# A decoder block on one core: three weight units instead of two in the program's first loads, from two queues

## The chip, the core and the metric

The kernel runs on one core of a Trainium2 chip. The core has five engines that run side by side: TensorE (PE in the profile; its weight loads are listed as PEld), VectorE (DVE), ScalarE (ACT), GpSimd (POOL) and SyncE (SP), which issues the transfers between HBM and the on-chip memory. Each engine works off its own list of instructions in order, and semaphores hold an instruction back until its operands are there. The metric is the device time of one execution in microseconds: 543.99 us, the median of three runs (543.96 to 544.42).

## The reference

One layer on 256 tokens of width 1024, in float32: a gated feed-forward block (width 2816), a mixing layer of two branches (attention over the tokens so far, and a spatial gating in chunks of 128), a second feed-forward block, and a last norm. The change touches the beginning, the first feed-forward block:

```python
def rmsnorm(x, g):
    y = xf * lax.rsqrt(jnp.mean(xf * xf, axis=-1, keepdims=True) + EPS)
    return (y * g.astype(jnp.float32)).astype(x.dtype)
def swiglu(x, w_gate, w_up, w_down):
    return (jax.nn.silu(x @ w_gate) * (x @ w_up)) @ w_down
h = h + 0.5 * swiglu(rmsnorm(h, ffn1_norm[l]), ffn1_w_gate[l], ffn1_w_up[l], ffn1_w_down[l])
```

## The kernel before

Every float32 operand of a product is split in two: a high part (the value cast to float32r) and a low part (the value minus its high part). A product is then high x high, high x low and low x high. The moving operand of the first feed-forward block is the input, turned (feature on the partitions, 256 tokens along the row), with its high and its low part side by side. So one product of 512 columns (`mm_high`, L159) gives high x high and high x low in two halves of a bank of PSUM, and one of 256 columns (`mm_low`, L164) adds low x high. `collect` (L189) brings a bank back: ScalarE copies the second half into a small buffer `lo` (of which there are two), and VectorE adds it to the first half.

Weights come in units. A unit of the first block (f1) holds 256 columns over all of K = 1024: 128 gate columns and the 128 up columns that belong to them, in 8 blocks of K. It takes 2 banks ("sides") and 2 x 8 products of either kind. Two rings hold weights: `rawp`, seven buffers of half a unit as loaded (512 KB each, SP issues them in order as buffers come free), and `wp`, four buffers of a whole unit, split (w0, w1, ... in the rows below; w4 takes the buffer of w0). `split` (L198) casts the high part on ScalarE (L199) and subtracts on VectorE (L200). `unit(i, ahead)` has units i to i + ahead split.

The first two units don't come that way. The array `first` in HBM holds the gain of the norm and, for each of the 8 blocks of K, the block's rows of the turned input (256 columns) and of the first two units (256 columns each). Seven pieces and a last one are loaded by SP in order (`load_front`, `CUTS`). For each block, ScalarE multiplies the input by the gain (L354, the high part), VectorE makes its low part (L355), and the two units are split. TensorE takes the blocks as they come: for each block, the four sides' high products and then the four sides' low products (`by_passes` with one block of K).

The input is multiplied by the gain alone at that point; the root mean square is applied behind the products. For it, the input comes once more in rows (tile h, L362), ScalarE squares it in four halves (`square_sum`, L233; tile sq), VectorE makes a mean for each 128 tokens (L240, L241; ms), GpSimd its power of -0.5 (L243; rstd), and TensorE turns the two columns rstd into a row over tokens (`rows_of`, L250; tile rows). These two turns stand in TensorE's list right behind the products of unit 3 and ahead of those of unit 4 (f1g4, f1u4). The results of units 0 to 3 wait in the tile `first` until the scale is there; from unit 4 on it is applied at once.

TensorE's and SP's lists are in the order in which the code is written. The lists of ScalarE, VectorE and GpSimd are put in order by a scheduler when the program is built, so an edit can move instructions that it doesn't name. Ahead of all, 14 products of zeros (`WARM`, L93) keep TensorE at work until the first data is there.

```python
for group in ((0, 1), (2,), (3,)):
    ...
    for ks in ([k] for k in range(KB)) if len(group) > 1 else (range(KB),):
        by_passes(sides, ks)
    for f, i in at:
        collect(first[:, f, i, :], ps[f, i])
rs = []
for j in range(NT):
    for hf in range(2):
        square_sum(h, j, hf, "1")
    rs.append(rstd_of(j, "1"))
rows = rows_of(rs, "1")
```

Of the kernel before, what the change touches and what calls it, by code (L numbers as in the profile page):

```python
# [32 lines left out]
FIRST = 2  # L33
# [6 lines left out]
CUTS = (0, 1, 2, 3, 4, 6, 7, 8)  # L40
# [3 lines left out]
def block_kernel(ctx, tc, t, out):  # L44
# [22 lines left out]

    ROW = S + FIRST * UC
    front = act.tile([P, FB * S], F32, tag="aTh", name="front")
    back = act.tile([P, ROW], F32, tag="nC", name="back")  # L70

    def load_front(k, end, c0=0, c1=ROW):

        a, b = KB * (k + c0 > 0) + k * ROW + c0, KB + (end - 1) * ROW + c1
        to = back[:, c0:c1] if k == KB - 1 else front[:, a:b]
        nc.sync.dma_start(to, t["first"][:, a:b])

    load_front(0, 1, 0, S + UC)
    load_front(0, 1, S + UC, ROW)
# [86 lines left out]
    def by_passes(sides, ks=range(KB)):  # L166
# [11 lines left out]
        if KB - 1 in ks:  # L178
            for ps, of in sides:
                (sh, _), both = of(KB - 1)  # L180
                mm_high(ps, sh, both, False, True)

# [26 lines left out]
    def block_of(nT, k):  # L209
        return both_of(nT, k)[:, 0, :], both_of(nT, k)[:, 1, :]  # L210
# [129 lines left out]
    def in_front(k, end):  # L340
        if k == KB - 1:
            return back.rearrange("p (k c) -> p k c", k=1)
        return front[:, KB + k * ROW:KB + end * ROW].rearrange("p (k c) -> p k c", k=end - k)

    for i in range(FIRST):
        unit_tile(i)
    for k, end in zip(CUTS, CUTS[1:]):
        if k:
            load_front(k, end)
        rows_of_k = in_front(k, end)  # L350
        for q in range(end - k):
            g = front[:, k + q:k + q + 1]
            hi, lo = block_of(nT, k + q)
            nc.scalar.activation(hi, rows_of_k[:, q, :S], AF.Identity, scale=g)  # L354
            nc.vector.scalar_tensor_tensor(lo, rows_of_k[:, q, :S], g, hi.bitcast(F32),  # L355
                                           op0=ALU.mult, op1=ALU.subtract)
        for i in range(2):
            w = parts[i]
            split(w[:, k:end, 0, :], w[:, k:end, 1, :], rows_of_k[:, :, S + i * UC:S + (i + 1) * UC])
# [5 lines left out]
    for group in ((0, 1), (2,), (3,)):  # L365
        at = [(f, i) for f in group for i in range(2)]
        w = {f: unit(f1 + f, PAIRED if len(group) > 1 else ALONE) for f in group}
# [3 lines left out]
        for ks in ([k] for k in range(KB)) if len(group) > 1 else (range(KB),):  # L371
            by_passes(sides, ks)
# [340 lines left out]
```

## Time and profile before

| | |
|---|---|
| median of 3 runs | 543.99 us (543.96 to 544.42) |
| the profiled execution | 544.41 us |
| its span, first to last instruction | 542.7 us |
| mean granted TensorE clock | 0.996 |
| PE, DVE, ACT busy | 533.7, 388.9, 304.3 us |
| moved by DMA | 103.04 MB, mean 190 GB/s |

The span is 1.7 us shorter than the execution's own time, which holds what lies around the first and the last instruction. Busy time is a mean over stages with other limits; the chain of work that ended last says which engine's work sets the end. Durations of products are modelled and overlap, so the rate of TensorE is read from the distance of one start to the next.

### The profile page before, as it was taken

The page shows a single profiled execution, that of the slowest core. Times are in us where ns is not written, and L with a number is a line of the kernel's source. Part 1 is how long each engine was busy: PE and PEld are TensorE (multiplying, and loading weights), DVE is VectorE, ACT ScalarE, POOL GpSimd, SP SyncE. Part 2 cuts the span into 40 slices and gives each one's busy share as a digit, 9 for nine tenths or more (in the row PEclk, how much of TensorE's full clock was granted, in tenths as well). Part 3 has the DMA queues.
Part 4 walks back from the last instruction along what each step waited for, and adds up shares of the span by engine and source line. Part 5 has one row for each costly group of instructions (what it writes and reads, how often), then busy time and mean ns, then how long its engine had stood idle before and what let it go on. Part 6 is the DMA issues. An engine that isn't in the chain of part 4 may idle for free.

```text
span 542.7 us, 8081 instructions
## 1 busy us (share of the span) xinstructions
PE 533.7 (98%) x3042; PEld 463.6 (85%) x3042; DVE 388.9 (72%) x627; ACT 304.3 (56%) x545; POOL 11.1 (2%) x25
## 2 busy tenths in 40 slices
PE   8999999999999999999999999999999999999995
PEld 6888888888888888888888998888888888888884
DVE  5979978787434676978896777787787878754323
ACT  6886556565434467457966544675655656552402
POOL 0000000000100010000000000000000000000002
PEclk9999999999999999999999999999999999999998
DMA  8977665557755468464265446476556555555002
GB/s 282 418 271 248 220 214 171 203 185 235 250 195 193 156 204 261 161 224 149 79 221 165 153 140 195 148 230 219 204 166 207 176 199 189 188 199 183 14 1 78
DMA packets 29143, 103.04 MB, mean 190 GB/s; under 512 B 3376, under 2 KB 3504, under 8 KB 29104
## 3 DMA queue, kind: packets, MB, share of 16 engines
q1 hardware_dynamic: 29104, 102.52, 55.7%
q8 instruction: 24, 0.39, 0.3%
q14 instruction: 15, 0.12, 0.1%
HBM read 101.46 MB, written 1.05 MB: 189 GB/s over the span
## 4 chain that ended last, share of the span: by engine, by line
PE 96%; DMA 1%; SPq 0%; ACT 0%; issue 0%; DVE 0%; POOLq 0%; DVEq 0%; POOL 0%; ACTq 0%
PE acch L186 9%; PE acch L185 9%; PE acch L187 9%; PE f2u L159 7%; PE f2g L159 7%; PE f1u L159 6%; PE f1g L159 6%; PE pgate L159 6%; PE f2u L164 4%; PE f2g L164 4%; PE f L159 3%; PE f1u L164 3%; PE f1g L164 3%; PE pgate L164 3%; PE pq L159 3%; PE f L164 2%
## 5 line engine op out<-in xcount | busy, mean ns | idle before, releaser
L200 DVE TENSOR_TENSOR w<-raw,w 128x1024 fp32r<-128x1024 f32 x180 | 216.6, 1219 | 58.0 <-ACT w L199 57.4
L199 ACT CAST w<-raw 128x1024 fp32r<-128x1024 f32 x180 | 181.4, 1055 | 59.8 <-PE acch L187 40.2
L159 PE MATMUL f2g<-n,w 128*128 128x512 f32 x160 | 62.7, 392 | 0.0
L159 PE MATMUL f2u<-n,w 128*128 128x512 f32 x160 | 62.6, 391 | 0.0
L159 PE MATMUL f1g<-n,w 128*128 128x512 f32 x144 | 56.3, 391 | 0.0
L159 PE MATMUL f1u<-n,w 128*128 128x512 f32 x144 | 56.3, 391 | 0.0
L164 PE MATMUL f2u<-n,w 128*128 128x256 f32 x160 | 39.2, 283 | 0.0
L164 PE MATMUL f2g<-n,w 128*128 128x256 f32 x160 | 39.1, 282 | 0.0
L186 PE MATMUL acch<-w,f2h 128*128 128x512 f32 (+1 forms) x110 | 38.3, 349 | 0.0
L185 PE MATMUL acch<-w,f2h 128*128 128x512 f32 (+1 forms) x110 | 38.3, 348 | 0.0
L187 PE MATMUL acch<-w,f2l 128*128 128x512 f32 (+1 forms) x110 | 38.1, 347 | 0.0
L164 PE MATMUL f1u<-n,w 128*128 128x256 f32 x144 | 35.3, 283 | 0.0
L164 PE MATMUL f1g<-n,w 128*128 128x256 f32 x144 | 35.2, 282 | 0.0
L159 PEld LDWEIGHTS f2u<-n,w 128*128 128x128 f32 x160 | 30.1, 188 | 5.7
L159 PEld LDWEIGHTS f2g<-n,w 128*128 128x128 f32 x160 | 30.1, 188 | 5.6
L159 PE MATMUL pgate<-n,w 128*128 128x512 f32 x128 | 34.7, 400 | 0.0
L185 PE MATMUL acch<-w,f1h 128*128 128x512 f32 x88 | 34.3, 390 | 0.0
L187 PE MATMUL acch<-w,f1l 128*128 128x512 f32 x88 | 34.3, 389 | 0.0
L186 PE MATMUL acch<-w,f1h 128*128 128x512 f32 x88 | 34.2, 389 | 0.0
L159 PEld LDWEIGHTS f1u<-n,w 128*128 128x128 f32 x144 | 27.1, 188 | 5.1
L159 PEld LDWEIGHTS f1g<-n,w 128*128 128x128 f32 x144 | 27.1, 188 | 5.0
L164 PEld LDWEIGHTS f2u<-n,w 128*128 128x128 f32 x160 | 30.6, 191 | 0.8
(186 smaller groups left out, 992.7 us busy)
## 6 DMA issues: line engine op xcount, KB each, us to landing
raw<-in_f SPq DMA_DIRECT2D x84, 512.0 KB, 4.9
raw<-in_f1d SPq DMA_DIRECT2D x22, 512.0 KB, 4.7
raw<-in_f2d SPq DMA_DIRECT2D x22, 512.0 KB, 4.5
raw<-in_gate SPq DMA_DIRECT2D x16, 512.0 KB, 4.5
raw<-in_qk SPq DMA_DIRECT2D x8, 512.0 KB, 5.3
raw<-in_out SPq DMA_DIRECT2D x8, 512.0 KB, 4.4
raw<-in_v SPq DMA_DIRECT2D x4, 512.0 KB, 4.8
raw<-in_gv SPq DMA_DIRECT2D x4, 512.0 KB, 4.8
```

The lines of the kernel that those rows point to most:

```text
L159: nc.tensor.matmul(ps, st, both.rearrange("p two n -> p (two n)"), start=first, stop=last)
L164: nc.tensor.matmul(ps[:, n:], st, both[:, 0, :], start=False, stop=False)
L185: nc.tensor.matmul(ps, sh, mh, start=first, stop=False)
L186: nc.tensor.matmul(ps, sh, ml, start=False, stop=False)
L187: nc.tensor.matmul(ps, sl, mh, start=False, stop=last)
L199: nc.scalar.copy(hi, src)
L200: nc.vector.tensor_sub(lo, src, hi.bitcast(F32))
```

## The change

`FIRST` becomes 3: the array `first` holds three units for each block of K (512 KB a block, with the input, where it was 384 KB). The first block comes in three pieces: the input's part (SP), unit 0's (issued by ScalarE, on its own queue), units 1 and 2 (SP). Block 1 is issued by ScalarE, blocks 2 to 7 by SP. The loads stand first in both lists. Blocks 5 to 7 land in the buffer that later holds the low parts of the block's result (aTl), where the last block before had a buffer of its own (nC).

For block 0 the high parts of units 0 and 1 are made by VectorE and that of unit 2 by ScalarE, ahead of the low parts, in a written order; TensorE begins with high x high of the six sides (256 columns each), then high x low, then low x high (`first_block`). From block 1 on it goes as before, with six sides. Units 0, 1 and 2 now form one group, unit 3 is the only one that stands alone, and `unit` is asked for one unit ahead in the group. The products are the same in number but for block 0's high ones, which are two of 256 columns instead of one of 512.

```diff
-FIRST = 2
+FIRST = 3
...
-CUTS = (0, 1, 2, 3, 4, 6, 7, 8)
...
+    def load_front(queue, k, c0=0, c1=ROW):
+        to = in_front(k)[:, c0:c1]
+        a, b = KB + k * ROW + c0, KB + k * ROW + c1
+        if k + c0 == 0:
+            a, to = 0, front[:, :b]
+        queue.dma_start(to, t["first"][:, a:b])
+
+    load_front(nc.sync, 0, 0, S)
+    load_front(nc.scalar, 0, S, S + UC)
+    load_front(nc.sync, 0, S + UC, ROW)
+    load_front(nc.scalar, 1)
+    for k in range(2, KB):
+        load_front(nc.sync, k)
...
+    def first_block(sides):
+
+        for q in range(2):
+            for ps, of in sides:
+                (sh, _), both = of(0)
+                nc.tensor.matmul(ps[:, q * S:(q + 1) * S], sh, both[:, q, :], start=q == 0, stop=False)
+        for ps, of in sides:
+            (_, sl), both = of(0)
+            mm_low(ps, sl, both)
...
+        if k:
+            x_high()
+            x_low()
+            for i in range(FIRST):
+                split(parts[i][:, k, 0, :], parts[i][:, k, 1, :], w[i])
+            continue
+
+        with tc.manual_schedule(engines={mybir.EngineType.DVE, mybir.EngineType.Activation}):
+            x_high()
+            for i in range(FIRST):
+                (nc.scalar.copy if i == FIRST - 1 else nc.vector.tensor_copy)(parts[i][:, k, 0, :], w[i])
+            x_low()
+            for i in range(FIRST):
+                nc.vector.tensor_sub(parts[i][:, k, 1, :], w[i], parts[i][:, k, 0, :].bitcast(F32))
...
-    for group in ((0, 1), (2,), (3,)):
+    for group in ((0, 1, 2), (3,)):
...
-        w = {f: unit(f1 + f, PAIRED if len(group) > 1 else ALONE) for f in group}
+        w = {f: unit(f1 + f, 1 if len(group) > 1 else ALONE) for f in group}
...
-        for ks in ([k] for k in range(KB)) if len(group) > 1 else (range(KB),):
+        if len(group) > 1:
+            first_block(sides)
+        for ks in ([k] for k in range(1, KB)) if len(group) > 1 else (range(KB),):
             by_passes(sides, ks)
```

The scheduler puts other lists together from this. Two places show it. The first is ScalarE's list around the squares of the input. Names with numbers: lo is the buffer of `collect`, f1_30 and f1_31 are the two banks of unit 3, w5_... and w6_... are split units (the number behind the underscore only tells tiles apart), raw6_1 is the second loaded half of unit 6, sq100 to sq111 are the squares of the two halves of tokens 0 to 127 (100, 101) and 128 to 255 (110, 111), rowsb1 the copy of the turned scale. Before:

```order
L192 COPY lo_334<-f1_20_300 128x256
L192 COPY lo_337<-f1_21_301 128x256
L199 CAST w5_289<-raw5_0_177 128x4x256
L233 ACTIVATE sq100_390,ss10_389<-h_78 128x512
L233 ACTIVATE sq101_392,ss10_389<-h_78 128x512
L233 ACTIVATE sq110_400,ss11_399<-h_78 128x512
L233 ACTIVATE sq111_402,ss11_399<-h_78 128x512
L192 COPY lo_383<-f1_30_349 128x256
L199 CAST w5_289<-raw5_1_187 128x4x256
L192 COPY lo_386<-f1_31_350 128x256
L252 COPY rowsb1_412<-rows1_409 128x256
```

and with the change:

```order
L212 COPY lo_342<-f1_21_224 128x256
L219 CAST w5_352<-raw5_1_201 128x4x256
L219 CAST w6_361<-raw6_0_203 128x4x256
L253 ACTIVATE sq100_413,ss10_412<-h_78 128x512
L212 COPY lo_406<-f1_30_372 128x256
L212 COPY lo_409<-f1_31_373 128x256
L253 ACTIVATE sq101_415,ss10_412<-h_78 128x512
L253 ACTIVATE sq110_423,ss11_422<-h_78 128x512
L219 CAST w6_361<-raw6_1_213 128x4x256
L253 ACTIVATE sq111_425,ss11_422<-h_78 128x512
L219 CAST w7_466<-raw7_0_217 128x4x256
L272 COPY rowsb1_435<-rows1_432 128x256
```

Before, the four squares stood together ahead of both copies of unit 3's banks. Now one square stands ahead of them and three behind, the last of these also behind a cast of unit 6. The second place is VectorE's list at the same point (first is the tile of units 0 to 3, ms10 and ms11 the two means, f1_30 and f1_31 as above). Before:

```order
L200 TENSOR_TENSOR w5_289<-raw5_0_177,w5_289 128x4x256
L240 TENSOR_TENSOR ms10_394<-ss10_389 128x1
L241 TENSOR_SCALAR ms10_394<-ms10_394 128x1
L240 TENSOR_TENSOR ms11_404<-ss11_399 128x1
L241 TENSOR_SCALAR ms11_404<-ms11_404 128x1
L196 TENSOR_TENSOR first_183<-f1_30_349,lo_383 128x256
L200 TENSOR_TENSOR w5_289<-raw5_1_187,w5_289 128x4x256
L196 TENSOR_TENSOR first_183<-f1_31_350,lo_386 128x256
```

and with the change:

```order
L220 TENSOR_TENSOR w5_352<-raw5_1_201,w5_352 128x4x256
L220 TENSOR_TENSOR w6_361<-raw6_0_203,w6_361 128x4x256
L216 TENSOR_TENSOR first_209<-f1_30_372,lo_406 128x256
L216 TENSOR_TENSOR first_209<-f1_31_373,lo_409 128x256
L260 TENSOR_TENSOR ms10_417<-ss10_412 128x1
L261 TENSOR_SCALAR ms10_417<-ms10_417 128x1
L220 TENSOR_TENSOR w6_361<-raw6_1_213,w6_361 128x4x256
L260 TENSOR_TENSOR ms11_427<-ss11_422 128x1
L261 TENSOR_SCALAR ms11_427<-ms11_427 128x1
```

Both means stood ahead of the sums of unit 3's banks and now stand behind them, and a subtraction of unit 6 (the second half) stands between the first mean and the second. On TensorE the two turns of the scale (L270 now) still stand between the last product of unit 3 and the first of unit 4. From unit 10 (f1g10) on, the lists of all engines stand in the same order as before.

## Rows read from the trace of the kernel before

**Rows 1.** The page of the profile: part 1 (busy time of an engine, share of the span, instructions) and part 4 (shares of the chain of work that ended last, by engine).

```profile
PE 533.7 (98%) x3042; PEld 463.6 (85%) x3042; DVE 388.9 (72%) x627; ACT 304.3 (56%) x545; POOL 11.1 (2%) x25
...
PE 96%; DMA 1%; SPq 0%; ACT 0%; issue 0%; DVE 0%; POOLq 0%; DVEq 0%; POOL 0%; ACTq 0%
```

**Rows 2.** The list of waits of TensorE (PE its products, PEld its weight loads): what waited <- what it waited for: us in total, times, longest us.

```profile
PE f L159 <- ACT w L199: 1.1, 3, 0.5
...
PEld f L159 <- ACT w L199: 2.5, 5, 0.8
```

**Rows 3.** The timeline of the first 40 us, rows of TensorE: start in us, length of the merged row in us, engine, line, operation, out<-in, shape, count, and in brackets the idle time before it and what ended it.

```profile
1.18 3.17 PE L93 MATMUL warm<-zeros 128*128 128x256 bf16 x14 [1.18 <-DVE zeros L90]
...
4.74 1.71 PE L159 MATMUL f<-n,w 128*128 128x512 f32 x4 [0.39 <-ACT w L199]
...
14.13 1.08 PE L159 MATMUL f<-n,w 128*128 128x512 f32 x4
...
29.45 0.38 PE L250 MATMUL rows<-ident,rstd 128*128 128x128 f32 x2
...
29.58 0.47 PE L159 MATMUL f1g<-n,w 128*128 128x512 f32 x1
```

**Rows 4.** The chain of work that ended last, 0 to 32 us, in order of time: start in us, us, what (merged rows; f is the tile of the first four units' products).

```profile
21.66 1.91 PE f L164 x16
23.57 3.65 PE f L159 x16
```

**Rows 5.** Busy time by stretch of 2 us. Each row: the stretch, its length, busy us of an engine with (x instructions), the granted TensorE clock, the mean busy share of the 16 DMA engines, GB/s.

```profile
0.00:2.00 2.00, 0.82 (x4) 0.58 (x5) 0.25 (x3) 1.21 (x1) 1.09 (x8) 1.00 0.13 10
2.00:4.00 2.00, 2.00 (x12) 1.36 (x9) 0.00 (x0) 0.71 (x4) 0.00 (x0) 1.00 0.86 218
4.00:6.00 2.00, 1.61 (x5) 1.10 (x4) 1.16 (x3) 0.68 (x3) 0.00 (x0) 1.00 0.85 270
6.00:8.00 2.00, 1.55 (x9) 1.20 (x9) 1.16 (x3) 1.11 (x3) 0.00 (x0) 1.00 1.00 341
8.00:10.00 2.00, 1.71 (x10) 1.36 (x9) 1.33 (x4) 1.87 (x6) 0.00 (x0) 1.00 0.99 389
```

**Rows 6.** The timeline, rows of ScalarE (ACT) that begin when a load has landed: the multiplication of a block of the input by the gain (L354).

```profile
3.57 0.51 ACT L354 ACTIVATE n<-front 128x256 fp32r<-128x256 f32 x1 [1.28 <-DMA front<-in_first]
...
6.21 0.51 ACT L354 ACTIVATE n<-front 128x256 fp32r<-128x256 f32 x1 [1.53 <-DMA front<-in_first]
...
8.13 0.51 ACT L354 ACTIVATE n<-front 128x256 fp32r<-128x256 f32 x1 [0.81 <-DMA front<-in_first]
```

**Rows 7.** Groups of instructions from 4 to 30 us by shape: line engine op, out<-in, shapes, count | busy us, mean ns of one | idle time before them and what ended it.

```profile
L200 DVE TENSOR_TENSOR w<-raw,w 128x1024 fp32r<-128x1024 f32 x7 | 8.4, 1222 | 0.6 <-ACT w L199 0.5
L199 ACT CAST w<-raw 128x1024 fp32r<-128x1024 f32 x8 | 8.1, 1060 | 0.0
L200 DVE TENSOR_TENSOR w<-front,w 128x256 fp32r<-128x256 f32 x10 | 3.8, 418 | 0.0
L199 ACT CAST w<-front 128x256 fp32r<-128x256 f32 x10 | 3.5, 396 | 0.0
L354 ACT ACTIVATE n<-front 128x256 fp32r<-128x256 f32 x7 | 3.4, 506 | 4.3 <-DMA front<-in_first 4.3
L355 DVE SCALAR_TENSOR_TENSOR n<-front,n 128x256 fp32r<-128x256 f32 x7 | 3.3, 482 | 5.9 <-ACT n L354 5.9
L196 DVE TENSOR_TENSOR first<-f,lo 128x256 f32<-128x256 f32 x7 | 2.8, 420 | 1.1 <-ACT lo L192 1.1
...
L192 ACT COPY lo<-f 128x256 f32<-128x256 f32 x7 | 2.3, 377 | 3.1 <-PE f L159 3.1
```

**Rows 8.** The timeline, three rows of two instructions each that ran end to end: start in us, length of the two together.

```profile
14.86 1.99 ACT L199 CAST w<-raw 128x1024 fp32r<-128x1024 f32 x2
...
18.23 0.76 DVE L196 TENSOR_TENSOR first<-f,lo 128x256 f32<-128x256 f32 x2
...
19.31 0.65 ACT L192 COPY lo<-f 128x256 f32<-128x256 f32 x2
```

**Rows 9.** The timeline, from the squares of the input to the scale that TensorE turns (sq: square with a sum, ms: mean, rstd: its power of -0.5).

```profile
25.34 0.63 ACT L233 ACTIVATE sq<-h 128x512 bf16<-128x512 f32 x1
...
26.09 0.63 ACT L233 ACTIVATE sq<-h 128x512 bf16<-128x512 f32 x1
...
27.61 0.63 ACT L233 ACTIVATE sq<-h 128x512 bf16<-128x512 f32 x1
...
28.36 0.16 DVE L240 TENSOR_TENSOR ms<-ss 128x1 f32<-128x1 f32 x1 [1.16 <-ACT sq L233]
...
28.79 0.55 POOL L243 TENSOR_TENSOR rstd<-ms,nhalf 128x1 f32<-128x1 f32 x1 [0.96 <-DVE ms L241]
```

**Rows 10.** The loads of the input in rows (tile h), 10 to 30 us: the issuing instructions with their duration and their first and last start, and us from issue to landing.

```profile
L362 SPq DMA_DIRECT2D h<-in_x x2: 328/328/328, 12.9 to 14.4; - x2
...
DMA to landing us min/median/max: 11.4/11.6/11.8
```

**Rows 11.** The timeline of TensorE at the end of the program: its last product.

```profile
535.84 0.28 PE L187 MATMUL acch<-w,f2l 128*128 128x256 f32 x1
```

**Rows 12.** Busy time by stretch of 1 us at the end, columns as in rows 5.

```profile
538.00:539.00 1.00, 0.00 (x0) 0.00 (x0) 0.55 (x2) 0.51 (x1) 0.42 (x1) 0.70 0.00 0
539.00:540.00 1.00, 0.00 (x0) 0.00 (x0) 0.20 (x1) 0.00 (x0) 0.00 (x0) 0.50 0.18 72
```

More of the change, by code (lines that the diff above doesn't have):

```diff
@@ L68, in block_kernel, with in_front @@
     ROW = S + FIRST * UC
+    TURN = 5
     front = act.tile([P, FB * S], F32, tag="aTh", name="front")
[L70 to L79, printed above, removed]
+    back = act.tile([P, FB * S], F32, tag="aTl", name="back")
+    def in_front(k):
+        return front[:, KB + k * ROW:KB + (k + 1) * ROW] if k < TURN else \
+            back[:, (k - TURN) * ROW:(k - TURN + 1) * ROW]
+    def load_front(queue, k, c0=0, c1=ROW):
[10 more added lines that the diff above has]
+        load_front(nc.sync, k)
     ident = consts.tile([P, P], F32, name="ident")
@@ L338, in block_kernel, with x_high, x_low @@
     nT = alloc_T("n1", ("nA", "nB"))
[L340 to L343, printed above, removed]
     for i in range(FIRST):
         unit_tile(i)
-    for k, end in zip(CUTS, CUTS[1:]):
-        if k:
[L349 to L359, printed above, removed]
+    for k in range(KB):
+        g, x = front[:, k:k + 1], in_front(k)[:, :S]
+        w = [in_front(k)[:, S + i * UC:S + (i + 1) * UC] for i in range(FIRST)]
+        hi, lo = block_of(nT, k)
+        def x_high():
+            nc.scalar.activation(hi, x, AF.Identity, scale=g)
+        def x_low():
+            nc.vector.scalar_tensor_tensor(lo, x, g, hi.bitcast(F32), op0=ALU.mult, op1=ALU.subtract)
+        if k:
+            x_high()
[10 more added lines that the diff above has]
+                nc.vector.tensor_sub(parts[i][:, k, 1, :], w[i], parts[i][:, k, 0, :].bitcast(F32))
     fetch_to(2 * FIRST + RAW)
```

## The prediction, as put on record before the changed kernel ran

> **What bounds the kernel now.** I read four views: the page for the engine that sets the end, the waits for its pauses, the timeline for the first 30 us, the stretches for the transfers. The page [rows 1] shows TensorE busy 98% of the span and 96% of the chain that ended last: what moves the end is a pause of TensorE, or the time at which its products begin. Its waits [rows 2] have one costly place, the first products: 2.5 us in five waits of a weight load, for ScalarE's casts of the blocks that came with the input. So I look at the stretch from the first product (4.74) to the first product of unit 4 (29.58) [rows 3]. Behind it I take TensorE to run as before: it had next to no wait there, and the other lists stand in their old order from unit 10 on.
>
> A unit has 16 products of 512 columns and 16 of 256. The chain shows 16 of each in 3.65 and 1.91 us [rows 4]: 5.56 us a unit, 22.2 for four. From 4.74 to the turn of the scale at 29.45 [rows 3] are 24.7 us, so 2.5 are pauses. That is all that an earlier and denser beginning can win, with what lies before 4.74.
>
> The seam that decides is the turn of the scale: two small products between unit 3 and unit 4, which need the squares of the input. Before, the last power ended on GpSimd at 28.79 + 0.55 = 29.34 [rows 9], the turn began at 29.45, and TensorE had just ended unit 3: no pause, and no slack either.
>
> **Step 1, the beginning.** The first product can't start before the 14 products of zeros end, 1.18 + 3.17 = 4.35 [rows 3], where it was 4.74. VectorE and ScalarE make the three high parts beside each other, then the low ones: with 0.4 to 0.5 us an instruction [rows 7], block 0's three passes of six 256-column products end at 7 to 7.5.
>
> Block 1 waits for its load. Before, pieces of 260, 128 and 384 KB had landed at 6.21, with another 384 KB at 8.13 [rows 6]. Now block 0 (516 KB) and block 1 (512 KB) are 1,028 KB; between the two points this gives 6.21 + 256/384 x 1.92 = 7.5. From bytes moved (2 x 10 + 2 x 218 + 2 x 270 = 996 KB by 6.0 [rows 5]) it could be there at 6.2. I take 6.9, the middle, since neither row tells what two queues do. Behind the landing stand the multiplication by the gain (0.51) and the low part beside the cast (0.48) [rows 7], and some 0.1 of signals: block 1's products begin at 8.0 (7.3 to 8.6).
>
> The Trainium skill, page "DMA: Bandwidth & Descriptors", section "Issuing engines are not separate DMA queues", says that transfers issued by several engines run on the same 16 DMA engines and interleave, so that a second issuer only saves issue time. The trace agrees so far: the 16 were 85 to 100% busy from 2 us on [rows 5]. By that rule block 1 shares with units 1 and 2 and block 2, and the landing is nearer to 7.5 than to 6.2: 0.6 us more than in my sum.
>
> From there I see no pause in the group: a block of three units is 3 x 5.56 / 8 = 2.09 us of products, against 0.51 + 3 x 0.40 = 1.7 on ScalarE, 0.48 + 3 x 0.42 = 1.7 on VectorE [rows 7], and 512 KB (0.524 MB) of a load in 1.35 us at the 389 GB/s of 8 to 10 us [rows 5]. The group ends at 8.0 + 7 x 2.09 = 22.6. Unit 3, whose halves are split by then, ends at 28.2, where it was 29.45: 1.25 us won.
>
> **Step 2, the squares.** In ScalarE's list (shown with the change) the work from the end of the group to the last square is now: six copies of banks, five casts of half units, one square, then the two copies of unit 3's banks, two squares, a cast, a square. In distances of starts a copy is 0.33, a cast 1.0 [rows 8], a square 0.76 [rows 9]. The first bank is complete about 1.0 us ahead of the group's end (five products behind it), at 21.6. Six copies (2.0), five casts (5.0) and the first square (0.76) last until 29.3, past unit 3's end. The two copies take it to 30.0, two squares to 31.5, the cast of unit 6 to 32.5, the last square to 33.3.
>
> VectorE's second mean stands behind the subtraction of that half of unit 6, which needs the cast: 32.55 + 1.22 [rows 7] = 33.8. Its two mean instructions took 0.43 until GpSimd could start (28.36 to 28.79 [rows 9]): 34.2. GpSimd's 0.55: 34.8. The turn and the first product of unit 4: 34.95, against 29.58 [rows 3]. Everything of TensorE that follows is late by **5.4 us**, the 1.25 of step 1 included. TensorE stands for 34.8 - 28.2 = 6.6 us but for the first of the two turns.
>
> Is another thing later still? VectorE's own list in that time is six sums (0.36 to 0.38 each [rows 8]) and five subtractions (1.22 [rows 7]), 8.4 us from about 22.1, and two more sums and a mean: done at 31.6, a microsecond ahead of the cast. The input in rows comes behind 1 MB more (a third unit) than before: two loads issued at 12.9 and 14.4 landed 11.8 and 11.4 us later [rows 10], at 24.7 and 25.8; 1.05 MB at 389 GB/s [rows 5] makes that 27.4 and 28.5. The first square stands at 28.6 and the third at 30.8, so the loads are covered by 1.2 and 2.3 us. If that cover went, each us of lateness beyond it would be one us more.
>
> Bounds of this step: with step 1's bounds the sum is +4.7 to +6.0; ScalarE's 7.7 us and the tail of 5.6 can be off by half a us together: +4.4 to +6.3. A loss cannot be excluded by other work: nothing but TensorE's own next products could fill the pause, and they stand behind the turn.
>
> **Step 3, the clock.** The 14 products of zeros took 3.17 us, 0.21 each for 256 columns [rows 3], where 256 columns later take 1.91/16 = 0.119 [rows 4]: the lower of the two levels, 1.2 GHz. (The column of the granted clock reads 1.00 in the first stretches [rows 5]; the distances contradict it, and I go by them.) The first four products of 512 columns still took 1.71 where later ones took 1.08 [rows 3]. So from its first product at 1.18 TensorE ran low until about 6.0, some 4.8 us. The other end of the program shows the fall: last product at 535.84 + 0.28 [rows 11], and the granted clock is 0.70 in the stretch 538 to 539 and 0.50 behind it [rows 12], a fall about 2.3 us after work ended. A pause of 6.6 us should therefore bring the lower level, and unit 4 begin on it. If the way back takes the 4.8 us of the start, and a product then costs 0.21 for 0.119, 4.8 x (1 - 0.119/0.21) = **2.1 us** are lost. The bounds are nothing (the clock holds) and 3.0 (it takes 6.8 us to return); I take the 2.1, the one rise that the trace has.
>
> The Trainium skill, page "TensorE: Matmul & The Clock Gate", section "HAM oscillation — how this bites in real kernels", says the same of idle gaps between groups of products: a gap that is long enough drops the clock, and every return is paid anew. No row of this trace has such a gap in the middle of the program; by that rule the sum with the 2.1 us is the right one, without it the first rival.
>
> **The sum.** The profiled execution: 544.41 + 5.4 + 2.1 = 551.9. The runs shown have their median 0.42 lower, 543.99, so I forecast 551.5 us for a median. Other edits I cost at nothing: the issue of two loads by ScalarE and the later load of its table lie ahead of the first landing (3.57 [rows 6]) on an engine that idles there; the buffer that block 5 to 7 land in is first needed for the results, behind the turn; the six banks of the group and unit 3's two leave none short, since the copies free the first ones early.
>
> **Rivals.**
> 1. The pause comes, but the clock holds, or returns at once: 544.0 + 5.4 = 549.4 (548.4 to 550.3). For it: the fall was seen once, at the end, when nothing followed. Against it: a pause three times as long as that fall took.
> 2. Faster: the squares are in time and only step 1 counts. Then unit 4 begins at 28.3 instead of 29.58, 542.7 us, at best 541.5 with all pauses gone. It would need ScalarE to end the last square before 27 us, that is to be done 6 us sooner than its list and its durations say. It decides from there: each us by which the last square misses 27 costs one, and at 28.3 the gain is used up.
> 3. Neither: the pause is there but only as long as the 1.25 won (544). No row speaks for that length.
> 4. The beginning is worse as well: the three loads in flight share so that block 1 lands at 8.5 or later, 1 us and more on top: 553 and above. For it: the slow 218 and 270 GB/s of the first 6 us [rows 5].
>
> **How the numbers follow.** Forecast (pause and low clock) 0.64, rival 1 0.23, rival 4 0.06, rival 2 0.04, rival 3 0.03. The forecast's own spread is 550 to 553 (4.4 to 6.3 with 1.5 to 2.8). With rival 1 the range is 548.6 to 553.0. A measurement of this kernel tells 0.2% (1.1 us) from no change. Faster 0.04, same 0.03, slower 0.93.
>
> **What would show it.** Right: first product near 4.4, block 1 near 8, unit 3 ending at 28 to 29; then in the waits a new long one of TensorE at the turn, 6 us or more, for GpSimd's second power; three squares behind the copies of unit 3's banks; a stretch near 35 to 39 us with a granted clock of 0.5; behind it no new waits, and all rows shifted alike. Wrong: rstd ready before unit 3 ends, the clock at 1.0 throughout, or a second long wait in the group for block 1 or 2.

## The result, and the profile after

The changed kernel takes 551.36 us, the median of four runs (551.05 to 553.06); the kernel before took 544.01 us on the same chip, the median of four. The ratio is 1.0139 (95% interval 1.0127 to 1.0151): slower by 7.4 us. The profiled execution took 551.36 us, its span is 549.6 (before 544.41 and 542.7), the mean granted clock 0.992.

The page of the changed kernel, part 1 and part 4, the lines that answer to [rows 1]:

```profile
PE 535.1 (97%) x3048; PEld 465.1 (85%) x3048; DVE 390.9 (71%) x637; ACT 304.7 (55%) x551; POOL 11.7 (2%) x25
...
PE 95%; ACT 1%; DVE 1%; DMA 1%; issue 0%; POOL 0%; POOLq 0%; DVEq 0%; SPq 0%; ACTq 0%
```

Nothing stands out there. Seven microseconds of 550 are hard to see in shares; the waits of TensorE show them. The waits of TensorE's products and of its weight loads in the changed kernel, answering to [rows 2]:

```profile
PE rows L270 <- POOL rstd L263: 6.1, 2, 3.7
...
PE f L198 <- DVE w L383: 1.0, 1, 1.0
...
PEld rows L270 <- POOL rstd L263: 6.8, 2, 4.1
```

The old waits for ScalarE's casts are gone. In their place stands one of a microsecond in block 0 and, for GpSimd's powers at the turn of the scale, 6.8 us in two pieces.

**The beginning.** The timeline of the changed kernel, 0 to 9 us, rows of TensorE, and two of VectorE and ScalarE that need a load; columns as in [rows 3]:

```profile
4.29 0.62 PE L198 MATMUL f<-n,w 128*128 128x256 f32 x2
...
5.59 0.29 DVE L383 CAST w<-front 128x256 fp32r<-128x256 f32 x1 [1.45 <-DMA front<-in_first]
...
5.94 1.46 PE L198 MATMUL f<-n,w 128*128 128x256 f32 x10 [1.03 <-DVE w L383]
...
6.14 0.51 ACT L368 ACTIVATE n<-front 128x256 fp32r<-128x256 f32 x1
...
7.23 0.88 PE L174 MATMUL f<-n,w 128*128 128x256 f32 x6
```

TensorE begins at 4.29 with unit 0's two sides. Then it stands until 5.94: units 1 and 2 of the same block land only at 5.59. Block 1's input, loaded from the other queue, is multiplied at 6.14 with no wait for its load, so it was there by then. The stretches say where the transfers' time went (columns as in [rows 5]):

```profile
2.00:4.00 2.00, 2.00 (x12) 1.36 (x9) 0.15 (x1) 1.53 (x3) 0.00 (x0) 1.00 0.93 282
4.00:6.00 2.00, 0.97 (x5) 0.51 (x3) 0.55 (x3) 0.60 (x2) 0.00 (x0) 1.00 1.04 383
```

By 5.59 some 2 x 7 (the stretch ahead of these) + 2 x 282 + 1.59 x 383 = 1,190 KB had moved. Block 0 needs 516 of them; the rest was for blocks that are needed later. Behind 7.95 block follows block in 2.1 us with no pause.

**The turn of the scale.** The timeline of the changed kernel, 27 to 36 us, from the end of unit 3 to the first products of unit 4 (answers to [rows 9] and to the last two of [rows 3]):

```profile
27.75 0.63 PE L169 MATMUL f<-n,w 128*128 128x512 f32 x2
28.04 0.67 ACT L253 ACTIVATE sq<-h 128x512 bf16<-128x512 f32 x1
...
28.66 0.67 ACT L212 COPY lo<-f 128x256 f32<-128x256 f32 x2
29.18 0.69 ACT L253 ACTIVATE sq<-h 128x512 bf16<-128x512 f32 x1
...
30.61 1.03 ACT L219 CAST w<-raw 128x1024 fp32r<-128x1024 f32 x1
...
31.43 0.55 POOL L263 TENSOR_TENSOR rstd<-ms,nhalf 128x1 f32<-128x1 f32 x1 [29.70 <-DVE ms L261]
31.55 0.63 ACT L253 ACTIVATE sq<-h 128x512 bf16<-128x512 f32 x1
31.67 1.22 DVE L220 TENSOR_TENSOR w<-raw,w 128x1024 fp32r<-128x1024 f32 x1 [0.33 <-ACT w L219]
...
33.00 0.15 DVE L261 TENSOR_SCALAR ms<-ms 128x1 f32<-128x1 f32 x1
33.23 1.64 POOL L263 TENSOR_TENSOR rstd<-ms,nhalf 128x1 f32<-128x1 f32 x1 [1.26 <-DVE ms L261]
33.24 1.23 DVE L220 TENSOR_TENSOR w<-raw,w 128x1024 fp32r<-128x1024 f32 x1
...
34.93 0.47 PE L270 MATMUL rows<-ident,rstd 128*128 128x128 f32 x1 [2.42 <-POOL rstd L263]
...
35.05 0.78 PE L169 MATMUL f1g<-n,w 128*128 128x512 f32 x1
...
36.05 0.63 PE L169 MATMUL f1g<-n,w 128*128 128x512 f32 x1
...
36.48 0.63 PE L169 MATMUL f1u<-n,w 128*128 128x512 f32 x1
```

TensorE has ended unit 3 at about 28.3, when the first square has hardly begun. The last square starts at 31.55, VectorE's second mean waits behind a subtraction of unit 6, and GpSimd's second power takes 1.64 us where the first took 0.55. Unit 4 begins at 35.05 instead of 29.58: 5.47 us late.

Its products then start 0.43 us apart (36.05, 36.48), where 512 columns took 0.23 in [rows 4]. The stretches of 1 us show the clock:

```profile
31.00:32.00 1.00, 0.00 (x0) 0.00 (x0) 0.64 (x4) 1.00 (x2) 0.55 (x1) 0.96 0.67 213
32.00:33.00 1.00, 0.48 (x1) 0.18 (x1) 0.97 (x2) 1.00 (x3) 0.00 (x0) 0.50 0.76 197
...
38.00:39.00 1.00, 1.00 (x4) 0.76 (x4) 1.00 (x4) 0.58 (x2) 0.00 (x0) 0.63 0.37 152
39.00:40.00 1.00, 1.00 (x6) 0.83 (x5) 1.00 (x4) 0.75 (x3) 0.00 (x0) 1.00 0.02 8
```

The granted clock falls to the lower level at 31.92 (0.92 of that stretch at 1.00 and the rest at 0.50 make its 0.96), some 3.6 us after unit 3 ended, and comes back at about 38.7. The last product of the program closes the account (answers to [rows 11]):

```profile
543.07 0.28 PE L207 MATMUL acch<-w,f2l 128*128 128x256 f32 x1
```

From the first product of unit 4 to the last one of the program are 543.07 - 35.05 = 508.02 us, where they were 535.84 - 29.58 = 506.26 [rows 3, 11]. So 1.76 us were lost behind the pause. That these are the low clock, and that nothing else in the 506 us moved, is tested in number 4. 5.47 + 1.76 = 7.23; behind the last product the tail is 0.3 shorter (549.6 - 543.07 = 6.53 against 6.86), which gives the 6.9 of the two spans. The tail's 0.3 lies between VectorE's last addition and ScalarE's last square (0.52 us from start to start for 0.80); its cause stays open.

### The profile page after: what moved, and what is told of

It is laid out like the page before. It is cut to its first block, busy times and chain, and to the rows that moved or that the text cites. A ratio compares the mean times of both kernels' runs of the same rounds, so it can differ in the third digit from the quotient of the medians.

```text
span 549.6 us, 8108 instructions
## 1 busy us (share of the span) xinstructions
PE 535.1 (97%) x3048; PEld 465.1 (85%) x3048; DVE 390.9 (71%) x637; ACT 304.7 (55%) x551; POOL 11.7 (2%) x25
## 4 chain that ended last, share of the span: by engine, by line
PE 95%; ACT 1%; DVE 1%; DMA 1%; issue 0%; POOL 0%; POOLq 0%; DVEq 0%; SPq 0%; ACTq 0%
PE acch L205 9%; PE acch L206 9%; PE acch L207 9%; PE f2u L169 7%; PE f2g L169 7%; PE f1u L169 6%; PE f1g L169 6%; PE pgate L169 6%; PE f2u L174 3%; PE f2g L174 3%; PE f1u L174 3%; PE f1g L174 3%; PE f L169 3%; PE pgate L174 3%; PE pq L169 3%; PE f L174 2%
## 5 line engine op out<-in xcount | busy, mean ns | idle before, releaser
L219 ACT CAST w<-raw 128x1024 fp32r<-128x1024 f32 x178 | 179.2, 1055 | 60.0 <-PE acch L207 40.2
L169 PE MATMUL f1g<-n,w 128*128 128x512 f32 x144 | 57.5, 399 | 0.0
```

Of the source, the lines that this page charges most:

```text
L169: nc.tensor.matmul(ps, st, both.rearrange("p two n -> p (two n)"), start=first, stop=last)
L219: nc.scalar.copy(hi, src)
```

## The experiments

Theory: an order in ScalarE's list costs 5.5 us (three squares behind the copies of unit 3's banks), and the low clock that follows the pause costs the other 1.8 (the tail gives 0.3 back). Rivals: the input in rows lands later and the order only follows from that; the low clock isn't what the second part is; GpSimd's long power is a part of its own.

**1. The order alone, in the kernel before.** Its three later squares are put behind both copies of unit 3's banks and nothing else is changed; loads, groups and the beginning stay.

```diff
     for j in range(NT):
         for hf in range(2):
-            square_sum(h, j, hf, "1")
+            with tc.issue_after((copied[0] if j + hf else copied[1]).ins):
+                square_sum(h, j, hf, "1")
...
```

The lines left out keep the two copies: copied[0] is ScalarE's copy of unit 3's last bank and copied[1] that of unit 2's.

> The kernel before with one order added: three of the four squares stand behind both copies of unit 3's banks in ScalarE's list, as they do with the change; loads, blocks and products as before. Theory (the order alone makes the loss): the casts of unit 6 come between the squares as well, the second power ends near 36.7, unit 4 begins at 36.9 instead of 29.58, the clock falls: 553 us (551 to 554). Rival (the loss comes from the third unit in the first loads): 544 to 545.

Measured: 554.12 us (553.7 to 555.34, four runs), 1.019 of the kernel before (1.0175 to 1.0205). The timeline of this kernel, GpSimd's second power and the product that begins unit 4:

```profile
35.40 1.63 POOL L245 TENSOR_TENSOR rstd<-ms,nhalf 128x1 f32<-128x1 f32 x1 [1.48 <-DVE ms L243]
...
37.21 0.77 PE L159 MATMUL f1g<-n,w 128*128 128x512 f32 x1
```

The order alone turns the kernel before into one that is slower than the changed one. Unit 4 begins 7.63 us late, more than the changed kernel's 5.47: the scheduler also puts a cast of a half unit behind each of the three (squares at 30.58, 32.14 and 33.70, casts at 31.21 and 32.77). From there to the last product (545.45) are 508.24 us, 1.98 more than in the kernel before: the low clock again (granted 0.50 until 41.4 us). With a tail that is 0.3 shorter here too, these make the 9.3 between the spans (552.0 and 542.7).

**2. The change with the input's rows loaded ahead of the raw weights.** In SP's list the two loads of h go in front of the first loads of half units; the scheduler then puts the four squares far ahead.

```diff
-    fetch_to(2 * FIRST + RAW)
     for j in range(NT):
         nc.sync.dma_start(h[:, j, :], t["x"][j * P:(j + 1) * P, :])
+    fetch_to(2 * FIRST + RAW)
```

> The changed kernel with the two loads of the input in rows issued ahead of the loads of unit 3 on, nothing else edited. The scheduler then puts the four squares in front of the casts of unit 3 in ScalarE's list. Theory (the loss is the place of the squares in the lists, and the low clock that follows): TensorE does not wait at the turn, unit 4 begins right behind unit 3, near 28.4 us instead of 35.05 (changed) and 29.58 (before), the granted clock stays at 1.00, 542.9 us (542.4 to 543.5). Rival A (the loss is in the beginning or anywhere else): 550 to 552. Rival B (weights that come 2.6 us later take the place of the wait): a new wait of 1 to 2.5 us at unit 3 or 4, 544 to 545.5.

Measured: 544.35 us (542.9 to 545.2, eleven runs), ratio 0.9998 (0.9988 to 1.0008). All of the 7 us are back with an edit of one line's place. GpSimd's second power in this kernel and, from the timeline of TensorE, the beginning and the first product of unit 4:

```profile
19.06 0.56 POOL L263 TENSOR_TENSOR rstd<-ms,nhalf 128x1 f32<-128x1 f32 x1 [0.67 <-DVE ms L261]
```

```profile
4.62 0.77 PE L198 MATMUL f<-n,w 128*128 128x256 f32 x2 [0.27 <-ACT n L368]
6.33 2.50 PE L198 MATMUL f<-n,w 128*128 128x256 f32 x10 [0.95 <-DVE w L383]
8.63 1.48 PE L174 MATMUL f<-n,w 128*128 128x256 f32 x6
...
30.42 0.47 PE L169 MATMUL f1g<-n,w 128*128 128x512 f32 x1
```

The powers are ready 10 us ahead, and TensorE's waits list none for the turn. But the gain of 1.25 us that an earlier beginning should have left isn't in the median: 544.35 is what rival B said, but the new wait at unit 3 or 4 that it needs isn't there. The eleven times lie in two groups, four at 542.90 to 543.13 and seven at 544.34 to 545.20, and the profiled execution (544.96) is of the upper one: its ten products at 6.33 took 2.50 us and the six behind them 1.48, where the changed kernel's took 1.46 and 0.88. From start to start the ten take 8.63 - 6.33 = 2.30 us here and 7.23 - 5.94 = 1.29 there, so 0.23 and 0.13 us for 256 columns: the two levels of the clock. That is a second effect, taken up in number 8.

**3. The loads as in number 2, the order as in number 1.** It tells the landing of h from the order.

> The changed kernel with the input's rows loaded ahead of unit 3 on and the same order added as in the run on the kernel before: three squares behind both copies of unit 3's banks, though their operand has landed 8 us earlier. Theory (the place in the list decides): unit 4 begins at 35 to 37, the clock falls, 551 to 554 us. Rival (the later landing of the input decides): 542.9, as the run with the input's rows first.

Measured: 553.11 us (552.3 to 554.97, four runs), ratio 1.0163 (1.0146 to 1.018). The input's rows are loaded first and it doesn't help: the powers run at 34.49, one behind the other, and unit 4 begins at 37.85. So the place in ScalarE's list decides, not when h lands. (Behind the pause are 508.86 us to the last product, 546.71, so the low clock took 2.60 here.) In the changed kernel itself the two loads landed 11.0 and 11.4 us after they were issued at 13.6 and 15.3: at 26.7 at the latest, where the first square was at 28.04.

```profile
34.49 3.18 POOL L265 TENSOR_TENSOR rstd<-ms,nhalf 128x1 f32<-128x1 f32 x2 [32.76 <-DVE ms L263]
```

**4. TensorE kept at work through the pause.** In the changed kernel, 48 products of zeros, written to a bank that nobody reads, stand between unit 3 and the turn.

```diff
+    fill = bank("fill")
+    for i in range(48):
+        nc.tensor.matmul(fill[:, :S], zeros[:, :P], zeros, start=True, stop=True)
     rows = rows_of(rs, "1")
```

> The changed kernel with 48 products of zeros (256 columns, 0.12 us each, 5.7 us) on TensorE between unit 3 and the turn of the scale; they write a bank that nothing reads. Theory (the pause lets the clock fall, and the way back costs 1.7 us): the pause in useful work stays, unit 4 still begins at 35.0, the granted clock stays at 1.00, 549.6 us (549.2 to 550.2), 1.7 less than the changed kernel. Rival (the low clock costs nothing, since something else holds the program after the pause): 551.3.

Measured: 549.67 us (549.52 to 551.63, four runs), ratio 1.0113 (1.0095 to 1.0131). From the timeline of TensorE in this kernel:

```profile
34.96 0.48 PE L169 MATMUL f1g<-n,w 128*128 128x512 f32 x1
35.27 0.40 PE L169 MATMUL f1u<-n,w 128*128 128x512 f32 x1
35.51 0.40 PE L169 MATMUL f1g<-n,w 128*128 128x512 f32 x1
```

The stretch in which unit 4 begins (columns as in [rows 5]), and the last product:

```profile
34.00:36.00 2.00, 1.12 (x6) 0.94 (x7) 1.90 (x3) 0.47 (x2) 0.82 (x1) 1.00 1.02 379
```

```profile
541.23 0.28 PE L207 MATMUL acch<-w,f2l 128*128 128x256 f32 x1
```

Unit 4 begins at the same time as in the changed kernel (34.96 for 35.05), but its products are 0.24 apart at once, and the granted clock is 1.00 in all stretches from 30 to 44 us. From there to the last product are 541.23 - 34.96 = 506.27 us, where the kernel before has 506.26: with the clock held, nothing of the 1.76 is left. The median comes down by 1.7 us. So the pause has two prices: its length and the clock behind it.

**5. The turn behind unit 4's products.** TensorE then has 5.6 us of work of its own in the place of the pause; unit 4's results wait for the scale like those of units 0 to 3.

```diff
+    w4 = unit(f1 + 4, ALONE)
+    ps4 = [bank(f"f1{'gu'[i]}4") for i in range(2)]
+    by_passes([(ps4[i], weights_of(w4, nT, i)) for i in range(2)])
     rows = rows_of(rs, "1")
...
```

> The changed kernel with the two turns of the scale moved behind unit 4's products in TensorE's list; loads and squares stay where the change put them. Theory: the squares are as late as before, but TensorE has 5.6 us of unit 4's products in the meantime; the second power is there at 34.9, unit 4 ends at 33.8, so about 1.1 us of waiting are left and the clock stays at 1.00: 543.8 us (543.3 to 544.4). Rival (the squares' lateness costs through the collecting, whatever stands on TensorE): 548 or more.

Measured: 545.78 us (544.01 to 546.95, twelve runs), ratio 1.002 (1.0009 to 1.0031). The timeline of TensorE at the turn:

```profile
33.78 0.27 PE L270 MATMUL rows<-ident,rstd 128*128 128x128 f32 x1
34.94 0.33 PE L270 MATMUL rows<-ident,rstd 128*128 128x128 f32 x1 [0.89 <-POOL rstd L263]
```

The wait of TensorE's products for the powers shrinks from 6.1 us to 0.9, and the granted clock is 1.00 in every stretch up to 44 us. By the medians 5.6 us of the loss are back, with the squares as late as before. What is left of the wait is GpSimd's long second power (33.25, 1.64 us). The times again lie in two groups, 544.01 to 544.32 (five runs, that with the trace among them) and 545.69 to 546.95 (seven); only the first group is where the theory had it.

**6. GpSimd's power without VectorE beside it.** In the changed kernel the second power began at 33.23 and a subtraction of VectorE at 33.24; the subtraction ended at 34.47 and the power at 34.87. The trace of the kernel before has one such pair, later in the program:

```profile
194.85 1.21 DVE L200 TENSOR_TENSOR w<-raw,w 128x1024 fp32r<-128x1024 f32 x1
```

```profile
195.01 1.46 POOL L243 TENSOR_TENSOR rstd<-ms,nhalf 128x1 f32<-128x1 f32 x1 [7.99 <-DVE ms L241]
```

Both times the power ends 0.40 to 0.41 us after VectorE's subtraction, as if it could only then begin. The Trainium skill, page "SBUF — State Buffer", section "SBUF: two separate sides", says that VectorE and GpSimd share a pair of ports as an exclusive lock, taken for a whole instruction, when a VectorE operation with two inputs in SBUF meets a GpSimd operation that reads SBUF. The traces agree, with 1.64 and 1.46 us against 0.55 alone, and a power that was well under way isn't delayed: that at 31.43 took its 0.55 though a subtraction began at 31.67. Which of the two came first at 33.23 and 33.24 can't be told from 0.01 us. The edit puts the split of unit 7, ScalarE's casts and VectorE's subtractions, behind the first multiplication by the scale (`scaled[0]`):

```diff
-                split(w[:, sl, 0, :], w[:, sl, 1, :], raws.pop((i, hf)))
+                if i == 7:
+                    with tc.issue_after(scaled[0].ins):
+                        split(w[:, sl, 0, :], w[:, sl, 1, :], raws.pop((i, hf)))
+                else:
+                    split(w[:, sl, 0, :], w[:, sl, 1, :], raws.pop((i, hf)))
...
```

> The changed kernel with VectorE's subtractions of unit 7 ordered behind the first multiplication by the turned scale, so that VectorE has nothing to do while GpSimd makes the second power. Theory (the second power took 1.64 us instead of 0.55 because VectorE's subtraction ran beside it): it takes 0.55 again, unit 4 begins at 33.9 to 34.0, the time is 1.1 us less, 550.3 (549.8 to 550.8). Rival (GpSimd is slow there for a reason of its own): 1.64 again and 551.4.

Measured: 551.2 us (551.15 to 552.29, four runs), ratio 1.0138 (1.0123 to 1.0153). The timeline of this kernel at the turn:

```profile
29.65 0.66 ACT L259 ACTIVATE sq<-h 128x512 bf16<-128x512 f32 x1
...
34.85 0.55 POOL L269 TENSOR_TENSOR rstd<-ms,nhalf 128x1 f32<-128x1 f32 x1 [1.26 <-DVE ms L267]
...
35.58 0.78 PE L175 MATMUL f1g<-n,w 128*128 128x512 f32 x1
```

The power is short, and the casts can't have made it long: in the changed kernel ScalarE ran nothing from 33.20 to 35.44. From the first square to unit 4 are 5.93 us, 1.08 less than the changed kernel's 7.01. The time didn't follow: 0.16 us less in the median. Part of it can be seen in this execution: from unit 4 to the last product (544.02) are 508.44 us, so the low clock took 2.18 and not 1.76. The rest stays open, since the one execution with a trace (552.29) had also begun late (its first square stands 1.6 us behind that of the changed kernel) and is 1.1 us above the other three. So the cause of the long power is shown, its worth in time isn't: the expected 550.3 was missed, and 551.2 is close to what the rival had.

**7. One queue, and block 0 like the others.** Two variants of number 2: all loads of the beginning issued by SP in order; and block 0 in the order of the other blocks, with 512-column products and without `first_block`.

```diff
-    load_front(nc.scalar, 0, S, S + UC)
+    load_front(nc.sync, 0, S, S + UC)
     load_front(nc.sync, 0, S + UC, ROW)
-    load_front(nc.scalar, 1)
+    load_front(nc.sync, 1)
```

```diff
-        if k:
+        if True:
             x_high()
...
-        if len(group) > 1:
-            first_block(sides)
-        for ks in ([k] for k in range(1, KB)) if len(group) > 1 else (range(KB),):
+        for ks in ([k] for k in range(KB)) if len(group) > 1 else (range(KB),):
```

> As the run with the input's rows first, and both loads that ScalarE issued go back to SyncE's queue, in the order in which the blocks are used. Theory (the load of units 1 and 2 for block 0 landed late, 5.59 us, because block 1 shared the DMA engines with it from the other queue): that load lands at 4.5 to 4.9, block 0's products end at 7.0 to 7.4 instead of 7.95, and block 1 begins when its load is there, 7.2 to 8.1: 0 to 0.7 us less than the run with two queues. Rival (two queues really fill the DMA engines earlier): block 1 begins at 8.2 or later, 0.3 us or more above that run.

> As the run with the input's rows first, but block 0 is treated as the other blocks: high products of 512 columns, high parts of the weights by ScalarE, no written order. Theory (the high parts alone let TensorE begin before the low parts, but what holds block 0 is the landing of units 1 and 2 at 5.59): first product 0.3 to 0.5 us later, block 0 ends 0.3 to 0.8 us later than 7.95, and all of that shows at the end, 0.3 to 0.8 us above the run with the input's rows first. Rival (the first block's order is worth nothing, since the load decides): within 0.2 us of it.

Measured: one queue 544.09 us (543.09 to 544.91, eleven runs), ratio 1.0 (0.9991 to 1.0009); block 0 like the others 543.09 (542.72 to 544.73, eleven runs), ratio 0.9989 (0.998 to 0.9998). With one queue, units 1 and 2 are there earlier: they land at 5.06 and TensorE resumes at 5.41, where the traces with two queues and the same order of block 0 have 5.89 to 6.33. So, as far as one trace tells, the second queue delays what is needed first. The medians don't tell it: in this execution the products are then at the low rate all the same, and block 1 begins at 8.98 and not by 8.1:

```profile
4.08 0.77 PE L198 MATMUL f<-n,w 128*128 128x256 f32 x2
5.41 2.50 PE L198 MATMUL f<-n,w 128*128 128x256 f32 x10 [0.56 <-DVE w L383]
```

That the plain block 0 would cost something was wrong: six of its runs are at 542.72 to 543.09, five at 544.06 to 544.73. The beginning with high parts alone buys nothing that these runs can tell.

**8. Why the times fall into two groups.** In every kernel with the changed beginning TensorE stands still for 0.6 to 1.0 us between 4.5 and 6.4 us, behind 14 products of zeros and two others (plain block 0: 0.70 ahead of these two as well). In the executions with a trace the products behind that pause ran either at the high rate within 1 us or at the low rate until 9 or 10 us. Theory: that pause is what lets the rise of the clock come late in some runs. Rival: the late rise is chance and has nothing to do with it. The test is the number of zeros alone (`WARM`): 20 in number 2 close the pause, 8 add one; 18 in the plain version close its first pause, 16 in the kernel before that kernel's first one, of 0.39 us.

> x_first with 20 products of zeros at the start instead of 14: at 0.213 us each they last until about 5.6, so the first product starts near 5.6 and the pause of 1.0 to 1.4 us in block 0 shrinks to 0.2 to 0.7. Block 0 needs its 18 products behind 5.6 and ends before or near 8.0, where block 1 begins now, so nothing is lost by the later first product. Theory (the pause at 4.6 to 6.3 us is what lets the rise of the clock come late): the clock stands at 1.0 from 4 us in every run, all times in the lower group of x_first, median 542.9 (542.6 to 543.3), no second group at 544.3. Rival (the late rise is chance and does not hang on the pause): two groups as before, median 543.5 to 544.5.

> x_first with 8 products of zeros instead of 14: they end near 2.9, so TensorE stands still for 1.3 us before the first product as well as for 1.3 us in block 0. Theory (pauses before 6 us make the rise late): the clock rises at 9 to 10 us in every run, median 544.6 (544.2 to 545.2), no run in the lower group at 542.9. Rival (chance): the two groups of x_first, median 544.0 to 544.4, some runs at 542.9.

> x_first_plain_block0 (block 0 in the order of the other blocks, 512-column products first) with 18 products of zeros instead of 14: they end near 5.0, where its first product starts now, so the pause of 0.7 us before it goes; the one of 0.67 us behind it stays. Theory: the rise is early in every run, the runs above 543.5 go, median 542.9 (542.6 to 543.2), 0.9977 of the kernel before. Rival: unchanged, median 543.1 with runs up to 544.7.

> The kernel before with 16 products of zeros instead of 14: they end near 4.75, where its first product starts, so its first pause of 0.39 us goes and the others stay. If this alone made the gain of the two kernels above, it would be faster too: theory: 543.7 to 544.1, no difference that can be measured, because its clock rises early already. Rival (more zeros help whatever the beginning): 543.0 or less.

Measured, eleven runs each, beside 543.99 us (543.70 to 544.36) for the kernel before on the same chip (number 2 ran on another, where the kernel before took 544.16):

| kernel | median | lowest to highest | ratio, 95% interval |
|---|---|---|---|
| number 2 with 20 zeros | 543.13 | 542.85 to 543.59 | 0.9985 (0.9976 to 0.9994) |
| number 2 with 8 zeros | 544.85 | 544.22 to 545.71 | 1.0018 (1.0009 to 1.0027) |
| plain block 0 with 18 zeros | 542.91 | 542.54 to 543.13 | 0.9979 (0.997 to 0.9988) |
| kernel before with 16 zeros | 543.91 | 543.58 to 544.64 | 0.9999 (0.999 to 1.0008) |

The timeline of TensorE, number 2 with 20 zeros:

```profile
1.18 4.45 PE L103 MATMUL warm<-zeros 128*128 128x256 bf16 x20 [1.18 <-DVE zeros L100]
5.28 2.34 PE L198 MATMUL f<-n,w 128*128 128x256 f32 x12
```

and with 8 zeros:

```profile
4.51 0.77 PE L198 MATMUL f<-n,w 128*128 128x256 f32 x2 [1.44 <-ACT n L368]
6.08 2.50 PE L198 MATMUL f<-n,w 128*128 128x256 f32 x10 [0.79 <-DVE w L383]
```

With the pause filled, every run (up to 543.59) is below the whole upper group of number 2 (from 544.34), although the first product starts 0.7 to 1.0 us later; with a longer pause every run is above the whole lower group, and the two rows are 1.7 us apart on one chip. By chance alone both groups would be expected in both rows: that rival is out. What these runs don't tell apart is the pause and the number of zeros, since an edit of `WARM` changes both; with 18 zeros in the plain version a pause of 0.43 us stays, and yet every run is at 543.13 or below. The kernel before gains nothing from two more zeros, so they repair a weakness of the new beginning.

The third row is the version that beats both kernels: input rows loaded first, block 0 in the plain order, 18 zeros. From its timeline:

```profile
4.78 0.71 PE L169 MATMUL f<-n,w 128*128 128x512 f32 x2
5.92 1.19 PE L169 MATMUL f<-n,w 128*128 128x512 f32 x4 [0.43 <-ACT w L219]
```

Its unit 4 begins at 28.06, 1.52 us ahead of [rows 3], and its median is 1.08 us below the kernel before.

## Why the prediction was right, point by point

The forecast (551.5 for 551.36), its mechanism and all three steps held in their signs; the sizes hold errors that cancel, so that the time was hit within 0.2 us is luck.

**Step 1, the beginning.** Values right, reason wrong. First product 4.29 (4.35 predicted), block 1 at 7.95 (8.0), unit 3's end about 28.3 (28.2). But block 1 didn't wait for its load, which I had landing at 6.9: it was there by 6.14, and block 0 was late instead, because its own units 1 and 2 landed at 5.59. I had block 0 end at 7 to 7.5 without asking when its last piece lands. The Trainium skill, page "DMA: Bandwidth & Descriptors", section "Issuing engines are not separate DMA queues", says that loads from several issuers interleave. The trace agrees, with the harm at another place than I put it: not block 1 behind the others, but block 0 behind block 1 (1,190 KB moved by 5.59 for its 516). Number 7 shows it from the other side: in one queue the products resume at 5.41 instead of 5.89 to 6.33.

**Step 2, the squares.** The mechanism is shown by numbers 1 to 3: the order in the list alone, whatever the landing. The sum was right to 0.1 us (unit 4 at 34.95, measured 35.05) by two errors of opposite sign. ScalarE was faster than I made it: I had taken half the length of a merged row of two as the distance of two starts, 0.33 for a copy and 1.0 for a cast. A row's length holds the tail of its last instruction, so the distance is the length less one mean: 0.65 - 0.377 = 0.27 and 1.99 - 1.06 = 0.93 [rows 7, 8]. With squares at 0.62 to 0.80 where I had 0.76 for each, the second power could begin at 33.23, and not at 34.2. GpSimd's second power was sized at the 0.55 of [rows 9] and took 1.64, since VectorE's next subtraction ran beside it; the price stood in the trace before (195.01, 1.46 us), but I had read only the power at 28.79.

**Step 3, the clock.** The fall and the return are there. 2.1 us were predicted and 1.76 measured, since the low level lasted 3.7 us behind the pause and not 4.8; number 4 removes it and gives 549.67, which is what my first rival had for a clock that holds (549.4). The price isn't one number: the four traces with such a pause have 1.76, 1.98, 2.18 and 2.60 us, with the low level lasting 3.7 to 5.6 us behind the pause. So 2.1 is a fair middle, and the 6.8 us of my upper bound had no row behind it. The Trainium skill, page "TensorE: Matmul & The Clock Gate", section "HAM oscillation — how this bites in real kernels", says that a long enough gap between groups of products drops the clock. The trace agrees, with 0.50 granted from 31.92 to 38.7; the price is the trace's.

**The rivals.** The second, faster with the squares in time, gave 542.7: number 2 reaches 542.9 to 543.1 in four of its eleven runs and, with zeros through the pause, in all within 543.6. What I had not seen is that the new beginning has a second outcome, 1.9 us slower (544.91 for 543.05, the medians of the two groups), most of it from the clock: in number 2's trace block 1 begins at 9.91 for 7.95, and of these 1.96 us the products' rate makes 1.57 and a later landing 0.39. The fourth, a worse beginning, is not what happened in the profiled execution; the one run at 553.06 lies 1.7 above the others, as the late rise of the clock would put it, but it has no trace.

**The sum.** 5.47 + 1.76 - 0.3 = 6.9 in the profiled execution, against 5.4 + 2.1 = 7.5. I also took 0.42 off for a median below the profile; the changed kernel's profiled execution was the median itself. The 0.3 of the tail was not foreseen.

## What to carry to other kernels

When an edit goes through a scheduler, read the new order of each engine's list at the seams where TensorE waits for a long chain: here a step that nobody edited made a pause of 6.7 us, five times the 1.2 us by which the edit had unit 3 end earlier, and moving two loads in the source took the pause away. A pause of TensorE is priced twice, by its length and by the clock behind it, and where the pause can't be removed, independent products in its place save the second price. When a load is split over two queues, give the second queue nothing that is needed later than what the first still carries: here that shows in the landing (one trace), not in the median.

## What the runs showed of the hardware that was not expected

- A pause of 0.6 to 1.0 us near 5 us, behind 14 products of zeros and two others, leaves the rise of the clock open: in some executions the 256-column products behind it start 0.13 us apart, in others 0.23 us apart until 9 or 10 us, and the program takes 1.9 us more (medians of the two groups of number 2). With 20 zeros all eleven times are those of an early rise, with 8 zeros those of a late one; one trace of each shows it. The column of the granted clock reads 1.00 in these stretches in either case, so only the distances show it.
- A single turn of 128 columns in the middle of the pause (32.03 in the changed kernel) didn't bring the clock back: it is at 0.50 from 32 to 38.7 us.
- The pause at the turn of the scale cost 1.76 to 2.60 us of low clock beside its own length, in four traces.
- A GpSimd operation on a 128x1 tile takes 1.46 to 1.64 us instead of 0.55 when a VectorE subtraction of 1.2 us starts with it or just before, and ends 0.4 us behind that; 0.55 when the subtraction starts 0.24 us later.
